# Five Strassen pairs in the longer down part, and an adding DMA for one weight piece of each gate/up chunk

## The chip, the cores and the metric

The kernel runs on one core of a Trainium2 chip, in float32 data. The metric is device time in microseconds (us), lower is better. The kernel before takes 1867.61 us (median of 3 runs, 1867.21 to 1868.33).

## The reference

One transformer layer on 256 tokens of width 2048, all in float32, cut to what matters here:

```python
def swiglu(h, w_gate, w_up, w_down):
    return (jax.nn.silu(h @ w_gate) * (h @ w_up)) @ w_down

def reference(x, positions, ...):
    x = x + 0.5 * swiglu(rmsnorm(x, ffn1_norm), w_gate1, w_up1, w_down1)   # 2048 -> 5632 -> 2048
    h = rmsnorm(x, mix_norm)
    ...   # projections of h, rope, retention, sparse attention -> ro, ao
    x = x + concatenate([ro, ao], axis=-1) @ w_out
    x = x + 0.5 * swiglu(rmsnorm(x, ffn2_norm), w_gate2, w_up2, w_down2)
    return rmsnorm(x, final_norm)
```

## The kernel before, in words

**Precision.** Each weight and each activation is split into a rounded part `hi` and a remainder `lo = raw - hi`. A product of two blocks is three matmuls (hi with hi, hi with lo, lo with hi), each of a 128x128 left block with 512 columns. ScalarE (ACT) writes `hi` (line 287), VectorE (DVE) writes `lo` (line 293).

**Pairs.** The large products go through `wide`. A chunk of 1024 output columns is worked off in pairs of weight rows (2 x 128 rows), one pair a load of 1 MB. A "C" pair makes eight block products, 24 matmuls, in two pieces of 12. An "S" pair makes seven products after Strassen and Winograd, 21 matmuls, in four pieces of 6, 6, 6 and 3; for it DVE forms four differences of weight blocks (`less`, line 279) and later recombines the seven sums. The left blocks of an S pair cost more too: `left_pair` makes four sums by `blocks_of` (lines 320 to 329) where a C pair has one split (lines 341 and 342), and it takes two tiles of the pool `mid` where a C pair takes one.

**A gate/up chunk** covers 512 hidden columns of gate and of up. Chunk 0 of each of the two FFNs has C pairs alone ("plain"); chunks 1 to 10 follow `UP` in the order S C S C S C C C, which is 22 pieces: 0 to 3 are the first S pair, 12 to 15 the third, 16 and 17, 18 and 19, 20 and 21 the three C pairs at the end (pair five, six and seven, counted from 0). The FFN runs in two parts: chunks 0 to 5, then the longer down part (`DOWN[0]`, 12 pairs for each half of the output), then chunks 6 to 10 and the shorter down part.

**Order.** Every engine works off its instructions in the order in which the program issues them, which is written out by hand. For step i the program first runs what is due at i (`run_step`), then issues `split(i + 4)`, the hi and lo of a piece four ahead, then the matmuls of piece i. Raw loads have three buffers and are issued by SyncE (SP) from `split`: on the first piece of load j, load j + 2 is issued, and it waits until the pieces of load j - 1 have been split. hi and lo have five buffers each. Things due: at step 16 of a chunk (`s_end`) `sums_of` begins: ACT copies bank M1 (line 482), DVE adds bank M6 to it (line 477). At step 17 TensorE (PE) turns the hidden values of the chunk before, four 128x128 transposes into M1 and four into M6 (line 567), so these wait for the copy and for the addition. At step 21 and at the next chunk's step 0, `ups` and `hidden` finish the chunk on DVE and ACT.

**Other places that the change touches.** `tables` makes the rope tables in two passes, one after the other, from the start of the first FFN's longer down part; `turn_early` turns x into four banks at the end of the first FFN; `row_of` and `scaled_tables` make a row of reciprocal norms and scale the tables with it; `ret_mix(3)` makes the last retention block for the output product; FIRST is the order of the first chunk's pairs, for each of which x is split, with more work for pairs 1, 3 and 5.

Of the kernel before, what the change touches and what calls it, by code (L numbers as in the profile page):

```python
# [19 lines left out]
P = 128  # L20
# [8 lines left out]
UP = "CSCSCSCC"  # L29
ORDER = (1, 0, 3, 2, 5, 4, 6, 7)  # L30
PLAIN = "CCCCCCCC"
FIRST = (0, 2, 4, 6, 7, 1, 3, 5)
DOWN = ("SCSCSCSCCCCC", "SCSCSCSCCC")
NH = 8
NI = 16
TOPK = 64
# [15 lines left out]
def layer(ctx: ExitStack, tc: tile.TileContext, a: dict, out: bass.AP):  # L52
# [2 lines left out]

    one = ctx.enter_context(tc.tile_pool(name="one", bufs=1))
    wts = ctx.enter_context(tc.tile_pool(name="wts", bufs=4))
    mid = ctx.enter_context(tc.tile_pool(name="mid", bufs=16))
    tmp = ctx.enter_context(tc.tile_pool(name="tmp", bufs=2))
    dram = ctx.enter_context(tc.tile_pool(name="dram", bufs=1, space=bass.MemoryType.DRAM))  # L60
    psum = ctx.enter_context(tc.tile_pool(name="psum", bufs=1, space=PSUM))
# [9 lines left out]
    def half_k(tag, bufs=2):  # L71
        return new(tmp, [P, 2, T], F32, tag, bufs)
# [35 lines left out]
    def after(step, fn):  # L108
        ends.setdefault(step, []).append(fn)
# [68 lines left out]

    def wide(src, plan, left, x0=False, tail=False, order=None, sums=SUM):

        start = len(pieces)
        seen, last = {}, {}
        ending = [[], []]
        s_end = None

        def mm(i, off, a, m, at=None, p=None):

            for n, (u, v) in enumerate(((0, 0), (0, 1), (1, 0))):
                st = m not in seen
                seen[m] = 1  # L190
                e = [i, off, (pieces[i]["pair"], a), m, u, v, st, False]
                last[m] = e
                pieces[i if at is None else at]["mms"].append(e)

        for at, p in enumerate(order or range(len(plan))):
            kind = plan[p]
            loads.append([(0, block(src, 2 * at, 2 * at + 2, 1024))])
            if x0:
                loads[-1] = [lambda p=p: load_xT(p)] + [(o, loads[-1][0][1][:, o:o + n]) for o, n in
                                                        ([(0, 512), (512, 512), (1024, 1024)] if at == 0 else [(0, 2048)])]  # L200
            i = len(pieces)
            if kind == "C":
                tiles = [(0, 1024), (1024, 1024)]
                if x0 and at == 0:
                    tiles = [(0, 512), (512, 512), (1024, 1024)]
            else:
                tiles = [(512, 1024), (1024, 1024), (0, 1024), (1536, 512)]
            for k, (off, n) in enumerate(tiles):
                pieces.append(dict(load=len(loads) - 1, off=off, n=n, mms=[], left=left, pair=p,
                                   sums=k if kind == "S" else None, x=[p] if x0 and k == 0 else []))  # L210
            if kind == "C":
                for c in (1, 0):
                    for k in range(2):
                        off = 1024 * (1 - c) + 512 * k
                        j = max(j for j, (o, n) in enumerate(tiles) if o <= off)
                        for t in range(2):
                            if tail and p >= len(plan) - 2:
                                ending[t].append((i + j, off - tiles[j][0], p, (t, k), sums[f"{t + 1}{c + 1}"]))
                                continue
                            mm(i + j, off - tiles[j][0], (t, k), sums[f"{t + 1}{c + 1}"])  # L220
            else:
                for k, off, a, m in S_BLOCKS:
                    mm(i + k, off, a, m)
                s_end = len(pieces)

        ending[1].sort(key=lambda e: e[4], reverse=True)
        for t in range(2):
            for i, off, p, a, m in ending[t]:
                mm(i, off, a, m, i if t == 0 else len(pieces) - 1)
        for e in last.values():  # L230
            e[7] = True
        return start, s_end, len(pieces) - 1, len(pieces)
# [22 lines left out]
        return len(pieces)  # L255

    n_loaded = [0]

    def load(i):
        raws[i] = new(wts, [P, 2048], F32, "raw", 3)  # L260
# [7 lines left out]
    def split(i):  # L268
        p = pieces[i]
        while n_loaded[0] < min(len(loads), p["load"] + 3):  # L270
            load(n_loaded[0])
            n_loaded[0] += 1
        for c in p.get("x", []):
            first_x(c, xT.pop(c))
        r = raws[p["load"]]
        raw = r[:, p["off"]:p["off"] + p["n"]]

        def less(a, b, o):
            V.tensor_tensor(r[:, o:o + 512], r[:, a:a + 512], r[:, b:b + 512], op=OP.subtract)  # L279


        k = p.get("sums")
        if k == 1:
            less(0, 1024, 1024)
        hi = new(wts, [P, 1024], F32R, "hi", BUFS)
        lo = new(wts, [P, 1024], F32R, "lo", BUFS)
        S.activation(hi[:, :p["n"]], raw, AF.Copy)  # L287
        if k == 1:
            less(0, 512, 0)
            less(512, 1024, 512)  # L290
        elif k == 2:
            less(1536, 512, 1536)
        V.tensor_tensor(lo[:, :p["n"]], raw, hi[:, :p["n"]].bitcast(F32), op=OP.subtract)  # L293
        split_of[i] = (hi, lo)


    def gain(norm, c, j):
# [141 lines left out]
    def row_of(tok):  # L439

        diag = new(tmp, [P, 2, P], F32, "diag", 1)
        for t in range(2):
            V.tensor_scalar(diag[:, t], ident, tok[:, t:t + 1], None, op0=OP.mult)
        ps = small()
        yield 2
        for t in range(2):
            TE.matmul(ps[:, t * P:(t + 1) * P], lhsT=ones, rhs=diag[:, t], start=True, stop=True)
        return ps[:, :T]
# [77 lines left out]
    def ffn(which, norm, next_norm, last):  # L526
        wgu, wd = a[f"wgu{which}"], [a[f"wd{which}{j}"] for j in range(2)]
        c = 0
        for part, n in enumerate(PARTS):
            hs = {}  # L530
            marks[which, part] = len(pieces)
            for cc in range(n):
                plain = c == 0
                start, s_end, half, end = wide(wgu[c], PLAIN if plain else UP, left_of(xg if plain else xs),
                                               plain and which == 1,
                                               order=ORDER if not plain else FIRST if which == 1 else None)
                u = {}

                if not plain:
# [51 lines left out]

    def turn_early(s_end, norm):

        for i, m in enumerate(("M1", "M5", "M6", "M7")):
            after(s_end + 2 + i, lambda i=i, m=m: turn_x(i, norm, m))

    def turn_late(end, norm, banks, later=0):
# [49 lines left out]

    rot_dram = new(dram, [P, 4, T], F32, "rot_dram")

    def tables():  # L650
        for k in range(2):
            ang, n = half_k("b"), half_k("sq")
            pi, pf = n[:, 0].bitcast(I32), n[:, 1]
            G.dma_start(pi, bass.AP(tensor=a["pos"].tensor, offset=a["pos"].offset, ap=[[0, P], [1, T]]))
            yield 4
            V.tensor_copy(pf, pi)
            for j in range(2):
                V.tensor_scalar(ang[:, j], pf, inv[:, k:k + 1], None, op0=OP.mult)
            yield 2
            V.tensor_scalar(n, ang, 1.0 / C_TWO_PI, None, op0=OP.mult)  # L660
            V.tensor_scalar(n[:, 0], n[:, 0], 0.25, None, op0=OP.add)
            yield 2
            V.tensor_scalar(n, n, MAGIC, None, op0=OP.add)
            V.tensor_scalar(n, n, MAGIC, None, op0=OP.subtract)
            for c in (C1, C2, C3):
                yield 2
                V.scalar_tensor_tensor(ang, n, -c, ang, op0=OP.mult, op1=OP.add)
            yield 1
            V.tensor_scalar(ang[:, 0], ang[:, 0], math.pi / 2, None, op0=OP.add)
            yield 1  # L670

            V.tensor_scalar(n, ang, 1.0 / C_TWO_PI, MAGIC, op0=OP.mult, op1=OP.add)
            V.tensor_scalar(n, n, MAGIC, None, op0=OP.subtract)
            for c in (C1, C2, C3):
                yield 2
                V.scalar_tensor_tensor(ang, n, -c, ang, op0=OP.mult, op1=OP.add)
            yield 2
            V.tensor_scalar(ang, ang, PI_DOWN, -PI_DOWN, op0=OP.min, op1=OP.max)
            yield 2
            S.activation(ang, ang, AF.Sin)  # L680
            yield 2
            V.tensor_scalar(ang[:, 1], ang[:, 1], sgn[:, k:k + 1], None, op0=OP.mult)
            G.dma_start(rot_dram[:, 2 * k:2 * k + 2], ang)
        yield 1
        act_table(AF.Silu)

    def load_tables():
        mix_ext()
# [12 lines left out]

    after(FIRST_SQ, first_squares)
    end = ffn(1, 0, 1, False)
    after(marks[1, 0, "down"] + 1, tables)
    after(marks[1, 1, "down"] + 4, load_tables)


# [6 lines left out]
        yield 2  # L714
        V.tensor_tensor(rot[:, :2], rot[:, :2], two(r_of[1]), op=OP.mult)

    after(m0 + 3, scaled_tables)

    heads = {}
    done_at = {}  # L720
# [26 lines left out]
    def cols(name, src, nchunks, idx=False, first=False):  # L747
# [7 lines left out]
        for c in range(nchunks):  # L755
# [3 lines left out]
            def done(chunk=chunk, c=c):  # L759
                if c % 2 == 0:  # L760
                    heads[name].append(big(shape=(P, 4, T)))
                return rope(chunk, 2, heads[name][c // 2][:, 2 * (c % 2):2 * (c % 2) + 2], idx,
                            3 if len(heads) == 1 and c == 0 else 1)

            after(end, done)
        done_at[name] = len(pieces)
# [42 lines left out]
    for c in range(4):  # L809
# [3 lines left out]
        def rg_done(chunk=chunk, c=c):  # L813
# [3 lines left out]
            s = half_k("s")  # L817
            S.activation(s, g, AF.Silu)
            gate[c] = s

        after(end, rg_done)
        rg_end.append(end)
# [213 lines left out]
    after(s + 6, ret_norm)  # L1036
    for n in range(2):
        after(s + 7 + n, lambda n=n: ret_scale(n))
    for c in range(4):
        after(max(rg_end[c] + 2, s + 10 + 2 * c), lambda c=c: ret_mix(c))  # L1040

    class MixIn:
# [129 lines left out]
```

## Time and profile before

| | |
|---|---|
| median of 3 runs | 1867.61 us |
| the profiled execution, its own time | 1868.15 us |
| its span, first to last instruction | 1866.3 us |
| busy: PE, DVE, ACT, POOL | 98%, 88%, 57%, 0% |
| granted TensorE clock | 0.997 of full speed |
| DMA engines busy with the loads of weights | 51.6% |

A busy PE counts pipelined matmuls whose ends are modelled, so the share says that PE hardly ever stops, not that it is at its peak. DVE is the engine with the next highest share. In rows of groups the columns are: line, engine, operation, out<-in, shapes, count, busy us, mean ns of one, and idle time before them with what ended it. In timelines: start, duration, engine, line, operation, and in brackets the idle time before it and its releaser.

### The profile page before, as it was taken

The numbers are of one execution on the slowest core, as the hardware profiler recorded it, in microseconds if no ns is written. First come the engines' busy times: TensorE is split into PE (matmuls) and PEld (weight loads), VectorE is DVE, ScalarE is ACT, GpSimd is POOL, SyncE is SP. The second block draws the span as 40 slices with busy tenths as digits, with TensorE's granted clock in tenths as the row PEclk, the third lists the DMA queues.
The fourth block names the chain that finished last, engine by engine and source line by source line (L and its number), as shares of the span: only waits on it lengthen the run. The fifth ranks groups of instructions, "written<-read, shape, count | busy, mean of one in ns | idle before, by whom it ended". The sixth has DMA issues, their size and how long they took to land.

```text
span 1866.3 us, 22800 instructions
## 1 busy us (share of the span) xinstructions
PE 1836.9 (98%) x8643; PEld 1523.8 (82%) x8643; DVE 1646.2 (88%) x2122; ACT 1072.9 (57%) x1353; POOL 6.9 (0%) x17
## 2 busy tenths in 40 slices
PE   9999999999999999999999999999999999999997
PEld 7788787888888887988888888888888888888886
DVE  6999999999999997689865886799999889999997
ACT  7655655545565555656554566556555455555564
POOL 0000000000000000000000000000000000000000
PEclk9999999999999999999999999999999999999999
DMA  8545555565554544545434464555555555555454
GB/s 316 203 181 183 203 203 191 180 229 198 205 206 183 212 181 173 184 159 210 179 137 172 145 225 150 207 185 191 210 207 183 202 203 198 186 188 212 186 190 170
DMA packets 52237, 360.51 MB, mean 193 GB/s; under 512 B 5984, under 2 KB 5984, under 8 KB 9632
## 3 DMA queue, kind: packets, MB, share of 16 engines
q1 hardware_dynamic: 50976, 355.62, 51.6%
q0 software_dynamic: 576, 1.84, 0.3%
q10 hardware_dynamic: 576, 1.60, 0.3%
q8 instruction: 67, 1.10, 0.2%
q14 instruction: 42, 0.34, 0.1%
HBM read 356.42 MB, written 2.62 MB: 192 GB/s over the span
## 4 chain that ended last, share of the span: by engine, by line
PE 80%; DVE 12%; ACT 4%; issue 2%; DMA 2%; SPq 0%; ACTq 0%; DVEq 0%
PE M L236 63%; PE M L150 8%; DVE lo L293 7%; PE M L152 4%; DVE raw L279 2%; ACT hi L287 2%; PE M L168 1%; PE M L169 1%; PE M L167 1%; PE M L567 1%; DMA raw<-in_wgu 1%; DMA e<-in_xT 1%; DVE x L474 1%; ACT sq L416 0%; DVE e L477 0%
## 5 line engine op out<-in xcount | busy, mean ns | idle before, releaser
L287 ACT ACTIVATE hi<-raw 128x1024 fp32r<-128x1024 f32 (+2 forms) x859 | 844.6, 1006 | 561.5 <-DVE raw L279 359.5
L293 DVE TENSOR_TENSOR lo<-raw,hi 128x1024 fp32r<-128x1024 f32 (+2 forms) x859 | 976.4, 1159 | 122.1 <-ACT hi L287 108.7
L236 PE MATMUL M<-hi,xg 128*128 128x512 f32 x2240 | 725.5, 390 | 1.7 <-ACT e L546 1.5
L236 PE MATMUL M<-hi,mid 128*128 128x512 f32 x1690 | 527.4, 391 | 1.9 <-DVE e L1001 1.6
L236 PEld LDWEIGHTS M<-hi,xg 128*128 128x128 f32 x2240 | 420.5, 188 | 89.2 <-ACT e L546 1.9
L236 PE MATMUL M<-lo,xg 128*128 128x512 f32 x1120 | 437.9, 391 | 5.7 <-DVE lo L293 5.6
L236 PEld LDWEIGHTS M<-hi,mid 128*128 128x128 f32 x1690 | 317.2, 188 | 70.2 <-DVE e L1001 2.0
L236 PE MATMUL M<-lo,mid 128*128 128x512 f32 x845 | 329.8, 390 | 1.0 <-DVE lo L293 0.8
L279 DVE TENSOR_TENSOR raw<-raw 128x512 f32<-128x512 f32 x380 | 262.9, 692 | 12.7
L236 PEld LDWEIGHTS M<-lo,xg 128*128 128x128 f32 x1120 | 210.3, 188 | 55.5 <-DVE lo L293 12.7
L150 PE MATMUL M<-xg,hi 128*128 128x512 f32 x688 | 245.6, 401 | 0.4 <-DVE xg L307 0.3
L236 PEld LDWEIGHTS M<-lo,mid 128*128 128x128 f32 x845 | 158.6, 188 | 36.5 <-DVE lo L293 4.3
L152 PE MATMUL M<-xg,lo 128*128 128x256 f32 x645 | 180.9, 280 | 0.0
L150 PEld LDWEIGHTS M<-xg,hi 128*128 128x128 f32 x688 | 128.7, 189 | 30.3 <-issue 1.3
L236 PE MATMUL M<-hi,ext 128*128 128x512 f32 x360 | 141.2, 392 | 1.5 <-ACT s L557 1.4
L152 PEld LDWEIGHTS M<-xg,lo 128*128 128x128 f32 x645 | 122.3, 190 | 0.8
L236 PEld LDWEIGHTS M<-hi,ext 128*128 128x128 f32 x360 | 67.5, 188 | 18.9 <-DVE s L477 3.6
L236 PE MATMUL M<-lo,ext 128*128 128x512 f32 x180 | 70.1, 389 | 0.0
L477 DVE TENSOR_TENSOR s<-s,M 128x512 f32<-128x512 f32 x98 | 65.6, 683 | 1.9 <-PE M L236 0.9
L557 ACT ACTIVATE s<-s,r_tok 128x512 f32<-128x512 f32 x40 | 27.0, 718 | 53.5 <-DVE s L477 53.5
L477 DVE TENSOR_TENSOR e<-s,M 128x512 f32<-128x512 f32 x58 | 39.7, 684 | 1.0
L742 ACT ACTIVATE b<-e 64x512 f32<-64x512 f32 (+2 forms) x46 | 28.1, 612 | 19.8 <-DVE e L728 19.3
(176 smaller groups left out, 933.2 us busy)
## 6 DMA issues: line engine op xcount, KB each, us to landing
raw<-in_wgu SPq DMA_DIRECT2D x175, 1024.0 KB, 4.8
raw<-in_wd SPq DMA_DIRECT2D x88, 1024.0 KB, 4.8
raw<-in_w_out SPq DMA_DIRECT2D x16, 1024.0 KB, 4.9
raw<-in_w_iq SPq DMA_DIRECT2D x8, 1024.0 KB, 4.8
raw<-in_w_aq SPq DMA_DIRECT2D x8, 1024.0 KB, 4.7
raw<-in_w_rk SPq DMA_DIRECT2D x8, 1024.0 KB, 4.8
raw<-in_w_rq SPq DMA_DIRECT2D x8, 1024.0 KB, 4.7
raw<-in_w_rv SPq DMA_DIRECT2D x8, 1024.0 KB, 4.9
```

The lines of the kernel that those rows point to most:

```text
L150: TE.matmul(acc, lhsT=hi[:, c:c + P], rhs=r, start=st, stop=sp)
L152: TE.matmul(acc[:, T:], lhsT=lo[:, c:c + P], rhs=r[:, :T], start=False, stop=False)
L167: TE.matmul(o, lhsT=h, rhs=hi[:, i * n:(i + 1) * n], start=st, stop=False)
L168: TE.matmul(o, lhsT=h, rhs=lo[:, i * n:(i + 1) * n], start=False, stop=False)
L169: TE.matmul(o, lhsT=l, rhs=hi[:, i * n:(i + 1) * n], start=False, stop=sp)
L236: TE.matmul(bank[m], lhsT=p["left"](pair, a)[u], rhs=split_of[i][v][:, off:off + 512], start=st, stop=sp)
L279: V.tensor_tensor(r[:, o:o + 512], r[:, a:a + 512], r[:, b:b + 512], op=OP.subtract)
L287: S.activation(hi[:, :p["n"]], raw, AF.Copy)
L293: V.tensor_tensor(lo[:, :p["n"]], raw, hi[:, :p["n"]].bitcast(F32), op=OP.subtract)
L477: V.tensor_tensor(o, a, b, op=OP.add)
L557: S.activation(u[b], bank[SUM[b]] if plain else u[b], AF.Silu, scale=r_tok[norm][:, t:t + 1])
L742: S.activation(b[p0:p0 + w], q[p1:p1 + w], AF.Copy)
```

## The change

- `DOWN[0]` has a fifth S pair (pair 8) in place of a C pair. It holds for both halves of the output in both FFNs. The pool `mid` gets a 17th tile, and the scratch of POOL's DMAs is set to 4096 bytes.
- In the twenty gate/up chunks that are not plain, the lo of the last piece (21) is no longer made by DVE. At `split(18)` ACT writes `-hi` of piece 21 into a new tile `lower`, and POOL issues a DMA that adds the raw piece to it.
- Orders and delays: FIRST; the banks of `turn_early`; `row_of` waits 3 steps in place of 2 and `scaled_tables` begins one step later, the first two ropes wait longer; `tables` runs as two chains, 28 and 57 steps after the start of the longer down part, each in fewer and fuller steps and with its own load of the Silu table; `ret_mix(3)` follows its gate directly.

```diff
-FIRST = (0, 2, 4, 6, 7, 1, 3, 5)
-DOWN = ("SCSCSCSCCCCC", "SCSCSCSCCC")
+FIRST = (0, 2, 1, 4, 3, 6, 5, 7)
+DOWN = ("SCSCSCSCSCCC", "SCSCSCSCCC")
...
-    mid = ctx.enter_context(tc.tile_pool(name="mid", bufs=16))
+    mid = ctx.enter_context(tc.tile_pool(name="mid", bufs=17))
...
+        if added:
+            pieces[-4]["lower"] = len(pieces) - 1
+            pieces[-1]["adds"] = True
...
         hi = new(wts, [P, 1024], F32R, "hi", BUFS)
-        lo = new(wts, [P, 1024], F32R, "lo", BUFS)
+        lo = lowers.pop(i) if p.get("adds") else new(wts, [P, 1024], F32R, "lo", BUFS)
         S.activation(hi[:, :p["n"]], raw, AF.Copy)
...
-        V.tensor_tensor(lo[:, :p["n"]], raw, hi[:, :p["n"]].bitcast(F32), op=OP.subtract)
+        if not p.get("adds"):
+            V.tensor_tensor(lo[:, :p["n"]], raw, hi[:, :p["n"]].bitcast(F32), op=OP.subtract)
         split_of[i] = (hi, lo)
+        if p.get("lower"):
+            q = pieces[p["lower"]]
+            src = raws[q["load"]][:, q["off"]:q["off"] + q["n"]]
+            lowers[p["lower"]] = t = new(wts, [P, 1024], F32R, "lower", 1)
+            S.activation(t, src, AF.Copy, scale=-1.0)
+            G.dma_start(t, src, accum_op=OP.add)
...
         ps = small()
-        yield 2
+        yield 3
...
-                                               order=ORDER if not plain else FIRST if which == 1 else None)
+                                               order=ORDER if not plain else FIRST if which == 1 else None,
+                                               added=not plain)
...
-        for i, m in enumerate(("M1", "M5", "M6", "M7")):
+        for i, m in enumerate(("M1", "M6", "M7", "M5")):
             after(s_end + 2 + i, lambda i=i, m=m: turn_x(i, norm, m))
...
-    def tables():
-        for k in range(2):
...
+    def tables(k):
+        ang, n = half_k("b"), half_k("sq")
...
+        S.activation(ang, ang, AF.Sin)
         yield 1
         act_table(AF.Silu)
+        yield 1
+        V.tensor_scalar(ang[:, 1], ang[:, 1], sgn[:, k:k + 1], None, op0=OP.mult)
+        G.dma_start(rot_dram[:, 2 * k:2 * k + 2], ang)
...
-    after(marks[1, 0, "down"] + 1, tables)
+    for k in range(2):
+        after(marks[1, 0, "down"] + (28, 57)[k], lambda k=k: tables(k))
...
-    after(m0 + 3, scaled_tables)
+    after(m0 + 4, scaled_tables)
...
-                            3 if len(heads) == 1 and c == 0 else 1)
+                            (5, 4)[c] if len(heads) == 1 and c < 2 else 1)
...
             gate[c] = s
+            if c == 3:
+                ret_mix(c)
...
-    for c in range(4):
+    assert rg_end[3] + 1 >= s + 16
+    for c in range(3):
         after(max(rg_end[c] + 2, s + 10 + 2 * c), lambda c=c: ret_mix(c))
...
-    nc = bacc.Bacc("TRN2", target_bir_lowering=False, num_devices=1)
+    nc = bacc.Bacc("TRN2", target_bir_lowering=False, num_devices=1, dynamic_dma_scratch_size=4096)
```

## Rows read from the trace of the kernel before

**Rows 1.** The page: busy time of each engine; the chain that ended last.

```profile
PE 1836.9 (98%) x8643; PEld 1523.8 (82%) x8643; DVE 1646.2 (88%) x2122; ACT 1072.9 (57%) x1353; POOL 6.9 (0%) x17
...
PE 80%; DVE 12%; ACT 4%; issue 2%; DMA 2%; SPq 0%; ACTq 0%; DVEq 0%
```

**Rows 2.** Waits of PE: who waited for whom, total us, times, longest us.

```profile
PE M L236 <- DVE lo L293: 6.4, 19, 0.7
PE M L447 <- DVE diag L443: 2.4, 1, 2.4
...
PE M L236 <- DVE e L1001: 1.6, 1, 1.6
PE M L236 <- ACT e L546: 1.5, 1, 1.5
PE M L405 <- DVE e L477: 1.4, 1, 1.4
PE M L236 <- ACT s L557: 1.4, 1, 1.4
```

**Rows 3.** Busy time by window: chunk 3, then the longer down part of FFN 1, FFN 2.

```profile
143.90:187.00 43.10, 42.76 (x193) 34.95 (x192) 41.46 (x51) 25.10 (x31) 0.54 (x1) 1.00 0.53 197
...
273.30:397.00 123.70, 121.46 (x536) 99.06 (x535) 118.17 (x153) 63.46 (x69) 1.63 (x3) 1.00 0.56 205
1413.00:1536.70 123.70, 123.70 (x552) 102.50 (x551) 109.06 (x122) 64.90 (x68) 0.00 (x0) 1.00 0.55 200
```

**Rows 4.** Timeline of PE around the start of chunk 3.

```profile
146.05 0.39 PE L236 MATMUL M<-hi,xg 128*128 128x512 f32 x1
146.78 0.50 PE L236 MATMUL M<-lo,xg 128*128 128x512 f32 x1 [0.34 <-DVE lo L293]
```

**Rows 5.** Groups by line and shape, DVE and ACT.

```profile
L293 DVE TENSOR_TENSOR lo<-raw,hi 128x1024 fp32r<-128x1024 f32 x756 | 910.4, 1221 | 117.7 <-ACT hi L287 104.3
L287 ACT ACTIVATE hi<-raw 128x1024 fp32r<-128x1024 f32 x756 | 783.0, 1056 | 477.6 <-DVE raw L279 293.1 <-PE M L236 112.6 <-PE M L169 21.2
...
L279 DVE TENSOR_TENSOR raw<-raw 128x512 f32<-128x512 f32 x380 | 262.9, 692 | 12.7
...
L293 DVE TENSOR_TENSOR lo<-raw,hi 128x512 fp32r<-128x512 f32 x97 | 66.4, 685 | 2.8 <-ACT hi L287 2.8
```

**Rows 6.** Chain that ended last: a long stretch of matmuls without a wait.

```profile
1449.56 156.43 PE M L236 x690
```

**Rows 7.** Timeline of ACT in chunk 3: hi of piece 18, copy of M1, hi of piece 20.

```profile
165.29 1.06 ACT L287 ACTIVATE hi<-raw 128x1024 fp32r<-128x1024 f32 x1 [0.29 <-PE M L236]
...
167.57 0.58 ACT L482 ACTIVATE s<-M 128x512 f32<-128x512 f32 x1
168.95 1.06 ACT L287 ACTIVATE hi<-raw 128x1024 fp32r<-128x1024 f32 x1 [0.80 <-DVE lo L293]
```

**Rows 8.** Timeline of SP in chunk 3: issue of the load of pieces 20 and 21.

```profile
164.07 0.33 SPq L266 DMA_DIRECT2D raw<-in_wgu  x1
```

**Rows 9.** DMA issues: engine, count, size, median us to landing.

```profile
raw<-in_wgu SPq DMA_DIRECT2D x175, 1024.0 KB, 4.8
...
mid<-in_qdec POOLq DMA_DIRECT2D x1, 512.0 KB, 6.8
```

**Rows 10.** Chain that ended last, chunk 3 of FFN 2: that load, then hi of piece 20.

```profile
1303.56 5.12 DMA raw<-in_wgu
...
1308.79 1.07 ACT hi L287
```

**Rows 11.** Timeline of DVE in chunk 3: the addition of M6.

```profile
168.84 0.68 DVE L477 TENSOR_TENSOR s<-s,M 128x512 f32<-128x512 f32 x1
```

**Rows 12.** Timeline of PE in chunk 3: the eight transposes and the matmul behind them.

```profile
169.81 1.03 PE L567 MATMUL M<-ident,e 128*128 128x128 f32 x8
170.60 0.48 PE L236 MATMUL M<-hi,xg 128*128 128x512 f32 x1
```

**Rows 13.** Chunk 7, where DVE ran early: hi of piece 20; PE's transposes and next matmul.

```profile
467.96 1.05 ACT L287 ACTIVATE hi<-raw 128x1024 fp32r<-128x1024 f32 x1
...
469.72 1.03 PE L567 MATMUL M<-ident,e 128*128 128x128 f32 x8
470.51 0.48 PE L236 MATMUL M<-hi,xg 128*128 128x512 f32 x1
```

More of the change, by code (lines that the diff above doesn't have):

```diff
@@ L177, in layer, with wide @@
         (3, 0, "A22", "M4"))
-    def wide(src, plan, left, x0=False, tail=False, order=None, sums=SUM):
+    def wide(src, plan, left, x0=False, tail=False, order=None, sums=SUM, added=False):
         start = len(pieces)
@@ L208, in wide @@
             for k, (off, n) in enumerate(tiles):
-                pieces.append(dict(load=len(loads) - 1, off=off, n=n, mms=[], left=left, pair=p,
+                pieces.append(dict(load=len(loads) - 1, off=off, n=n, mms=[], left=left, pair=p, lower=None, adds=False,
                                    sums=k if kind == "S" else None, x=[p] if x0 and k == 0 else []))
@@ L257, in layer @@
     n_loaded = [0]
+    lowers = {}
     def load(i):
@@ L648, in layer @@
     rot_dram = new(dram, [P, 4, T], F32, "rot_dram")
-    def tables():
-        for k in range(2):
[L652 to L683, printed above, removed]
@@ new lines, in tables, with less_turns @@
+    def tables(k):
+        ang, n = half_k("b"), half_k("sq")
+        pi, pf = n[:, 0].bitcast(I32), n[:, 1]
+        G.dma_start(pi, bass.AP(tensor=a["pos"].tensor, offset=a["pos"].offset, ap=[[0, P], [1, T]]))
+        yield 2
+        def less_turns(c):
+            V.scalar_tensor_tensor(ang, n, -c, ang, op0=OP.mult, op1=OP.add)
+        V.tensor_copy(pf, pi)
+        for j in range(2):
+            V.tensor_scalar(ang[:, j], pf, inv[:, k:k + 1], None, op0=OP.mult)
+        yield 1
+        V.tensor_scalar(n, ang, 1.0 / C_TWO_PI, None, op0=OP.mult)
+        V.tensor_scalar(n[:, 0], n[:, 0], 0.25, None, op0=OP.add)
+        yield 1
+        V.tensor_scalar(n, n, MAGIC, None, op0=OP.add)
+        V.tensor_scalar(n, n, MAGIC, None, op0=OP.subtract)
+        yield 1
+        less_turns(C1)
+        less_turns(C2)
+        yield 1
+        less_turns(C3)
+        V.tensor_scalar(ang[:, 0], ang[:, 0], math.pi / 2, None, op0=OP.add)
+        yield 1
+        V.tensor_scalar(n, ang, 1.0 / C_TWO_PI, MAGIC, op0=OP.mult, op1=OP.add)
+        V.tensor_scalar(n, n, MAGIC, None, op0=OP.subtract)
+        yield 1
+        less_turns(C1)
+        less_turns(C2)
+        yield 1
+        less_turns(C3)
+        V.tensor_scalar(ang, ang, PI_DOWN, -PI_DOWN, op0=OP.min, op1=OP.max)
+        yield 2
+        S.activation(ang, ang, AF.Sin)
@@ L684, in tables @@
         yield 1
         act_table(AF.Silu)
+        yield 1
+        V.tensor_scalar(ang[:, 1], ang[:, 1], sgn[:, k:k + 1], None, op0=OP.mult)
+        G.dma_start(rot_dram[:, 2 * k:2 * k + 2], ang)
     def load_tables():
```

## The prediction

> **What bounds the kernel now.** I read the busy shares and the chain first. PE is busy 98% of the span and holds 80% of the chain; DVE is busy 88% and holds 12% [rows 1]. So the time is PE's work plus the few places where PE stops, and almost all of these stops end on DVE. Second, the list of PE's waits: one small wait that recurs, DVE's lo, 19 times with 0.7 us at most, and single waits of 1.4 to 2.4 us at lines 447, 1001, 546, 405 and 557 [rows 2]. Third, the windows: in a gate/up chunk PE has 42.76 us of 43.1 and DVE 41.46, so DVE is all but full there; in the longer down part DVE has 118.17 us of 123.7 in the first FFN, where the rope tables are made, and 109.06 in the second, where they are not [rows 3]. Last, the timeline at the start of a chunk: the matmul with the lo of piece 4 starts 0.73 us after the one before it, where 0.23 is usual, a stop of 0.5 us [rows 4]. In the timeline this stop follows sixteen of the twenty chunks (1 to 4 and 7 to 10 of both FFNs): DVE leaves the end of a chunk, with the sums and the hidden values in it, about that late. It is what the adding DMA is aimed at.
>
> **The fifth S pair.** It removes 3 matmuls for each of two halves in two FFNs, 12 in all. A long stretch ran 690 matmuls in 156.43 us, 0.227 us each [rows 6], so PE is given back **2.7 us**. DVE gets four differences of 0.692 us and 1.5 more lo pieces (1.22 and 0.685): 4.7 us a pair, 9.4 us for each FFN's down part [rows 5]; ACT gets 1.5 hi pieces and has room (57%) [rows 1]. In the second FFN 109.06 + 9.4 = 118.5 us fits into 123.7 - 1.4 = 122.3 [rows 3]: no cost; the cover there is DVE's idle time. The pair's left blocks add sums and splits of some 2 us to DVE in one chunk of each FFN, in the place where DVE loses a lo of 1.22 us; I put that at nothing and let the bounds hold it.
>
> **The tables.** In the first FFN 118.17 + 9.4 = 127.6 us of DVE stands against 122.3 of PE. DVE is short by 5.3 us, and the two chains are put into the tails behind the last S pair of each half, where the recombining and the additions to x already stand, in some thirteen steps each where there were over twenty. I take **+6 us**, near the shortfall, because DVE won't work without any pause; the ends are 0, if the lead with which DVE leaves the part pays for all of it, and 11, if DVE keeps the 5.5 us of idle time that it has now [rows 3].
>
> **The adding DMA: what it gives.** DVE loses one lo of 1.22 us in each of twenty chunks, ACT gains one copy of 1.06 [rows 5]. The 0.5 us stops go, since DVE comes 1.2 us earlier to a place where it is 0.5 late: 16 x 0.5 = **-8 us**.
>
> **The adding DMA: what it costs.** The copy of -hi for piece 21 is issued by split(18), so it stands on ACT behind hi of piece 18 and ahead of hi of piece 19 and the copy of bank M1. It reads the load of pieces 20 and 21. In chunk 3 that load is issued at 164.07 [rows 8] and takes 4.8 us [rows 9]: it lands at 168.9. The chain shows the same in the second FFN: the load, 5.12 us, then hi of piece 20 0.1 us behind [rows 10]. Yet hi of piece 18 ends at 166.35, and the copy of M1 runs at 167.57, before the load has landed; hi of piece 20 starts at 168.95 [rows 7], as soon as it has (the view names DVE's lo there, but the landing is the later). So the new copy can't start before 168.95, and all behind it on ACT waits: 168.95 + 1.06 for it, 1.06 for hi of piece 19, then on DVE, which works in order too, 1.22 for lo of piece 19 and 0.68 for the addition of M6 [rows 5, 11]: 172.97. Today that addition ends at 169.52, just ahead of the eight transposes, whose second half needs it. The transposes take 0.79 us [rows 12]; half of them after 172.97 let the next product start at 173.4 in place of 170.60: PE stops for 2.8 us. In chunk 7, where DVE ran early, the same sum is 467.96 + 1.06 + 1.06 + 1.22 + 0.68 + 0.4 = 472.4 against 470.51 [rows 13]: 1.9 us. The ends are 1.9 and 2.8; with a lo less DVE will run like the early case, so I take 2.0. The load can't come much sooner: its buffer comes free with lo of piece 15, and from the chunk's start to there DVE is full with work that the change leaves alone. Transposes stand at that step in chunks 1 to 5 and 7 to 10 (chunk 6 follows the down part and has none), 18 in all: 18 x 2.0 = **+36 us**.
>
> The Trainium skill, in "PSUM — Partial Sum Buffer", section "Engine vs sequencer instructions", says that the queues of ScalarE and VectorE are strictly first in, first out. By that rule the 36 us stand; were it otherwise they would be nought. No row here shows an instruction overtaking another, and none shows one that could have.
>
> **The DMA itself.** No row shows an adding DMA. POOL's load of 512 KB took 6.8 us [rows 9]; an add reads two sides, so between 6.8 and twice that, 13.6. The copy ends at 170.0; PE wants piece 21's lower part after four more pieces of 12 matmuls, at 173.4 + 4 x 2.72 + 0.2 = 184.5: 14.5 us of cover, so nothing at either end, and I take 6.8. Behind it on SP stands the load that reuses that buffer, for pieces 6 to 9 of the next chunk; it would be issued at 177 to 184 and land 4.8 us later, and it is first read at about 189. POOL itself has 17 busy instructions in the whole span [rows 1], and no one waits behind it.
>
> The Trainium skill prices such a DMA lower ("DMA: Bandwidth & Descriptors", section "Anatomy of one DMA — SWDGE (gpsimd) path"): about 2 us and the bytes at 436 GB/s, an estimate of 3.2 us for 512 KB. The row is twice that; by the page the sum would be the same, with more cover.
>
> **The orders.** Each is priced by the wait that it can remove [rows 2]. turn_early: M5 is freed last and is now used last, -1.4 (line 405). The norm row: its matmul comes two steps, some 5 us, later, -2.4 (line 447); the ropes that follow have their own waits lengthened. ret_mix(3) stands ahead of a split on DVE, -1.6 (line 1001). FIRST: the work on x for pairs 1, 3 and 5 is spread, so the two waits of 1.5 and 1.4 at the end of chunk 0 (lines 546, 557) shrink; the Silu table load that sits between them stays, so I take half, -1.5. Together **-6.9 us**, with 0 as the other end, since a wait that goes may come back at the next instruction.
>
> **Sum.** 1868.15 (the profiled execution's own time) + 36 - 8 - 2.7 + 6 - 6.9 = 1892.6. The median of the runs is 0.5 us lower, so **1892 us**, 1.3% slower.
>
> **The rivals.**
> (a) The copy doesn't hold PE up: the load lands earlier than I think relative to ACT, or the transposes have other slack. Then the 36 us fall away: 1867.6 - 8 - 2.7 + 6 - 6.9 = 1856. For it: DVE, which frees the load's buffer, is relieved. Against it: hi of piece 20, which reads the same load, starts on the landing in chunk 3 of both FFNs, in the first 2.6 us after hi of piece 18 ended [rows 7, 8, 10]. It decides once the landing comes before the end of hi of piece 18. Chance 0.13.
> (b) The DMA is late: three passes instead of two make 20.4 us, 5.9 more than the cover, in each of twenty chunks: +118, about 2010. For it: nothing shows its speed, and it shares the engines with loads. Against it: 52% of the engines' time is used. Chance 0.06.
> (c) The wait is at its lower end, the tables fit, and the small ones give all they can, with further waits that I can't see shrinking: 1867.6 + 18 x 1.9 - 8 - 2.7 - 6.9 = 1884, and it takes 0.7 us less per chunk still to come within 0.2% of no change. That margin of 0.2%, 3.7 us, is about what a measurement of this kernel can tell. Chance of "same" 0.06.
>
> **How the numbers follow.** The forecast has 0.75, and with (b) slower has 0.81; faster 0.13; same 0.06. The forecast's own range is 1884 to 1867.6 + 18 x 2.8 - 8 - 2.7 + 11 = 1918. To hold the time 8 times in 10 it is taken down to 1867, through (c) and the same case; (a) and (b) are left out.
>
> **What would show it.** In the changed kernel PE should wait for DVE at line 477 some 18 times for about 2 us, and the recurring wait for lo of piece 4 should be gone; ACT's new copy should start on the landing of the load, 2 us after hi of piece 18. The down part of the first FFN should hold new waits for DVE in its two tails; the waits at lines 447, 405 and 1001 should be gone. I am wrong if the transposes of a chunk start as soon as the matmuls ahead of them end, or if the adding DMA lands after piece 20.

## The result and the profile after

The changed kernel takes **1898.12 us** (median of 4 runs, 1897.58 to 1899.25) against 1867.58 before (4 runs): ratio 1.0162, 95% interval 1.0149 to 1.0174, 30.5 us slower. Its profiled execution spans 1896.4 us, at a granted clock of 0.994 (0.997 before).

Lines of the code have moved: the split is now L291 (hi) and L298 (lo), the copy of -hi L304 and its DMA L305, the copy of bank M1 L493, the additions of sums L488, the additions to x L485, the transposes of a chunk L579, the matmuls of `wide` L239, those of a projection L150 and L152.

The page of after, busy time and the chain that ended last (before: [rows 1]):

```profile
PE 1840.0 (97%) x8631; PEld 1526.0 (80%) x8631; DVE 1642.0 (87%) x2136; ACT 1102.5 (58%) x1386; POOL 24.5 (1%) x37
...
PE 61%; DVE 26%; DMA 5%; issue 5%; ACT 3%; SPq 0%; ACTq 0%; DVEq 0%
```

PE's share of the chain fell from 80% to 61% and DVE's rose from 12% to 26%, though DVE has 4 us less to do. So it is not work that was added; somebody waits. The waits of PE say for whom (before: [rows 2]; who waited for whom, total us, times, longest us):

```profile
PE M L579 <- ACT s L493: 16.5, 18, 1.3
PE M L579 <- DVE s L488: 12.9, 18, 0.7
PE M L239 <- DVE x L485: 8.1, 3, 5.9
PE M L150 <- DVE xg L318: 4.2, 1, 4.2
PE M L239 <- DVE lo L298: 2.4, 5, 0.9
...
```

The waits for lo went from 19 to 5. In their place the transposes wait 18 times for the copy of M1 and 18 times for the addition of M6, 29.4 us in all. (The list counts idle time after a matmul's modelled end, so it holds somewhat less than PE loses.) Two more are new: 5.9 us for an addition to x, and 4.2 us for a turned tile of x at the projections. The first two are seen on ACT in chunk 3 (timeline; before: [rows 7]; in square brackets the idle time ahead of the instruction, and who ended it):

```profile
165.79 1.06 ACT L291 ACTIVATE hi<-raw 128x1024 fp32r<-128x1024 f32 x1 [0.29 <-PE M L239]
168.83 1.06 ACT L304 ACTIVATE lower<-raw 128x1024 fp32r<-128x1024 f32 x1 [1.97 <-DMA raw<-in_wgu]
169.80 1.04 ACT L291 ACTIVATE hi<-raw 128x1024 fp32r<-128x1024 f32 x1
170.74 0.58 ACT L493 ACTIVATE s<-M 128x512 f32<-128x512 f32 x1
```

and on PE (timeline; before: [rows 12]):

```profile
170.08 0.39 PE L239 MATMUL M<-hi,xg 128*128 128x512 f32 x1
171.37 0.66 PE L579 MATMUL M<-ident,e 128*128 128x128 f32 x4 [0.91 <-ACT s L493]
172.75 0.66 PE L579 MATMUL M<-ident,e 128*128 128x128 f32 x4 [0.72 <-DVE s L488]
173.16 0.47 PE L239 MATMUL M<-hi,xg 128*128 128x512 f32 x1
```

The copy starts on the landing, 1.97 us after ACT had nothing else ahead of it. hi of piece 19 and the copy of M1 need nothing from that load, yet they stand behind it. The Trainium skill ("PSUM — Partial Sum Buffer", section "Engine vs sequencer instructions") calls these queues strictly first in, first out; this trace agrees, with hi of piece 19 at 169.80 right behind the copy. On PE the eight transposes, one run before, are split into two fours with a stop ahead of each.

The period of a chunk is read from the copy of M1: its first and last start over chunks 1 to 5 (one line of code on ACT; copies, durations in ns, first and last start), before:

```profile
L482 ACT ACTIVATE s<-M x5: 576/578/580, 81.3 to 253.9; 128x512 f32<-128x512 f32 x5
```

and after:

```profile
L493 ACT ACTIVATE s<-M x5: 576/577/577, 81.9 to 259.7; 128x512 f32<-128x512 f32 x5
```

(253.9 - 81.3) / 4 = 43.15 us became (259.7 - 81.9) / 4 = 44.45, 1.3 more a chunk: the wait's cost less what the DMA gives. The same reading from chunk 5 to chunk 6 holds the longer down part of the first FFN: 253.9 to 426.0 before, 172.1 us; 259.7 to 442.3 after, 182.6.

### The profile page after: what moved, and what is told of

Its sections match the earlier page's. It is cut to its first block, busy times and chain, and to the rows that moved or that the text cites. A ratio compares the mean times of both kernels' runs of the same rounds, so it can differ in the third digit from the quotient of the medians.

```text
span 1896.4 us, 22945 instructions
## 1 busy us (share of the span) xinstructions
PE 1840.0 (97%) x8631; PEld 1526.0 (80%) x8631; DVE 1642.0 (87%) x2136; ACT 1102.5 (58%) x1386; POOL 24.5 (1%) x37
## 4 chain that ended last, share of the span: by engine, by line
PE 61%; DVE 26%; DMA 5%; issue 5%; ACT 3%; SPq 0%; ACTq 0%; DVEq 0%
PE M L239 42%; DVE lo L298 15%; PE M L150 9%; DVE raw L283 7%; DMA raw<-in_wgu 5%; PE M L152 4%; ACT hi L291 2%; DVE x L485 1%; DVE s L488 1%; PE M L168 1%; PE M L169 1%; PE M L167 1%; PE M L579 1%; DVE e L488 1%; ACT sq L427 0%
## 5 line engine op out<-in xcount | busy, mean ns | idle before, releaser
L291 ACT ACTIVATE hi<-raw 128x1024 fp32r<-128x1024 f32 (+1 forms) x867 | 856.2, 1006 | 518.3 <-DVE raw L283 362.0
L298 DVE TENSOR_TENSOR lo<-raw,hi 128x1024 fp32r<-128x1024 f32 (+1 forms) x847 | 960.8, 1155 | 157.0 <-ACT hi L291 142.3
L239 PE MATMUL M<-hi,xg 128*128 128x512 f32 x2240 | 726.5, 390 | 5.9 <-DVE x L485 5.9
L239 PE MATMUL M<-hi,mid 128*128 128x512 f32 x1682 | 527.1, 391 | 2.7 <-DVE x L485 2.3
L239 PEld LDWEIGHTS M<-hi,xg 128*128 128x128 f32 x2240 | 421.0, 188 | 93.2 <-DVE x L485 6.3
L239 PE MATMUL M<-lo,xg 128*128 128x512 f32 x1040 | 405.4, 390 | 0.8 <-DVE lo L298 0.7
L239 PEld LDWEIGHTS M<-hi,mid 128*128 128x128 f32 x1682 | 316.3, 188 | 72.2 <-DVE x L485 6.4
L239 PE MATMUL M<-lo,mid 128*128 128x512 f32 x841 | 328.5, 391 | 1.7 <-DVE lo L298 1.7
L283 DVE TENSOR_TENSOR raw<-raw 128x512 f32<-128x512 f32 x396 | 274.1, 692 | 13.3
L150 PE MATMUL M<-xg,hi 128*128 128x512 f32 x688 | 246.5, 402 | 4.2 <-DVE xg L318 4.2
L239 PEld LDWEIGHTS M<-lo,xg 128*128 128x128 f32 x1040 | 195.6, 188 | 41.6 <-DVE lo L298 1.6
L239 PEld LDWEIGHTS M<-lo,mid 128*128 128x128 f32 x841 | 158.2, 188 | 36.3 <-DVE lo L298 4.2
L152 PE MATMUL M<-xg,lo 128*128 128x256 f32 x645 | 181.5, 281 | 0.0
L150 PEld LDWEIGHTS M<-xg,hi 128*128 128x128 f32 x688 | 129.3, 189 | 34.1 <-DVE xg L318 4.6
L239 PE MATMUL M<-hi,ext 128*128 128x512 f32 x360 | 140.5, 390 | 0.7 <-ACT s L569 0.7
L152 PEld LDWEIGHTS M<-xg,lo 128*128 128x128 f32 x645 | 122.9, 190 | 0.7
L239 PEld LDWEIGHTS M<-hi,ext 128*128 128x128 f32 x360 | 67.7, 188 | 15.5 <-ACT s L569 1.1
L239 PE MATMUL M<-lo,ext 128*128 128x512 f32 x180 | 70.0, 389 | 0.0
L488 DVE TENSOR_TENSOR s<-s,M 128x512 f32<-128x512 f32 x98 | 65.2, 683 | 1.0
L579 PE MATMUL M<-ident,e 128*128 128x128 f32 x176 | 27.7, 284 | 29.4 <-ACT s L493 16.5
L579 PEld LDWEIGHTS M<-ident,e 128*128 128x128 f32 x176 | 18.8, 140 | 41.7 <-ACT s L493 22.4
```

The lines of the kernel that those rows point to most:

```text
L150: TE.matmul(acc, lhsT=hi[:, c:c + P], rhs=r, start=st, stop=sp)
L152: TE.matmul(acc[:, T:], lhsT=lo[:, c:c + P], rhs=r[:, :T], start=False, stop=False)
L239: TE.matmul(bank[m], lhsT=p["left"](pair, a)[u], rhs=split_of[i][v][:, off:off + 512], start=st, stop=sp)
L488: V.tensor_tensor(o, a, b, op=OP.add)
L579: TE.transpose(v[:, j, t * P:(t + 1) * P], ht[t][:, halves(2 * q + j, P)], ident)
```

## The experiments

Each time below stands against the runs of the kernel before on the same chip (1867.1, 1866.8 and 1867.75 us in the three sets). In the expectations W is the theory that ACT, waiting for the landing, holds up what is queued behind it; its rivals, B and D, put the cost on the new work itself, ACT's copy and the DMA's traffic. All edits are to the changed kernel where nothing else is said.

**The copy two pieces later**

```diff
-            pieces[-4]["lower"] = len(pieces) - 1
+            pieces[-2]["lower"] = len(pieces) - 1
```

> The changed kernel with one edit: the copy of -hi and the adding DMA for piece 21 are issued by the split of piece 20, behind its hi, in place of piece 18. Theory W (the copy holds ACT until its load has landed, and the transposes wait behind it): the copy now stands behind an instruction that waits for the same load anyway; the 18 waits of 1.07 + 0.86 us go, and 1898 falls by 34.7 to 1863 us (1860 to 1867). Theory B (what costs is ACT's extra 1.06 us and the added instructions, wherever they stand): 1898 within 3. Theory D (the adding DMA costs, by its traffic or by coming late): 1898 or more, since it now ends later and nearer to its use.

Measured 1861.70 us, ratio 0.9970 (0.9958 to 0.9982), inside W's range and 36.4 us less than after. The same copies and the same DMAs, issued at split(20), where hi of piece 20 has had to wait for that load anyway. ACT's timeline in chunk 3:

```profile
162.85 1.06 ACT L291 ACTIVATE hi<-raw 128x1024 fp32r<-128x1024 f32 x1 [0.25 <-PE M L239]
163.82 0.57 ACT L493 ACTIVATE s<-M 128x512 f32<-128x512 f32 x1
164.55 1.06 ACT L291 ACTIVATE hi<-raw 128x1024 fp32r<-128x1024 f32 x1 [0.16 <-DMA raw<-in_wgu]
165.52 1.04 ACT L304 ACTIVATE lower<-raw 128x1024 fp32r<-128x1024 f32 x1
```

The copy of M1 now comes ahead of the landing, and no wait of PE at L579 is left. W holds, and B and D, which leave the time at 1898, fall.

**The copy where it was, from a load that has landed** (it reads the load of its own piece 18; so one product of piece 21 takes another remainder)

```diff
-            src = raws[q["load"]][:, q["off"]:q["off"] + q["n"]]
+            src = raws[p["load"]][:, q["off"]:q["off"] + q["n"]]
```

> The changed kernel, with the copy and the adding DMA at the split of piece 18 as they are, but both read piece 19's half of the load that is already there in place of piece 21's; so one of the three products of the last piece of twenty chunks takes a wrong remainder. Same instructions, same places, same sizes, only no wait for a landing. Theory W: 1863 us (1860 to 1867). Theories B and D: 1898 within 3, since ACT's work and the DMA's traffic are all there.

Measured 1861.42 us, 0.9968 (0.9955 to 0.9981). The copy stands at split(18), ahead of hi of piece 19 as in the change, and costs nothing there once its data is in. So the cost is the wait for the landing alone, and not the copy, its place or the DMA.

**The copy with its wait, no DMA**

```diff
-        lo = lowers.pop(i) if p.get("adds") else new(wts, [P, 1024], F32R, "lo", BUFS)
+        lo = new(wts, [P, 1024], F32R, "lo", BUFS)
...
-        if not p.get("adds"):
+        if True:
...
-            G.dma_start(t, src, accum_op=OP.add)
```

> The changed kernel without the adding DMA: ACT's copy stays at the split of piece 18 and waits for the load of pieces 20 and 21, nobody reads it, and DVE makes the lo of piece 21 again. Theory W: the waits stay, and since DVE is as late as in the kernel before, each may grow from 1.9 to 2.8 us: 1898 to 1914. Theory D: the time falls to 1863 to 1875. Theory B: 1898 plus up to 10 for the stops on DVE that come back.

Measured 1922.39 us, 1.0295 (1.0280 to 1.0310), 24.3 us over after. Without the DMA's relief the small waits for lo come back, and the wait for the copy grows. PE's waits (the lines behind the DMA's stand one higher here):

```profile
PE M L578 <- ACT s L492: 21.0, 18, 1.5
PE M L578 <- DVE s L487: 12.9, 18, 0.7
...
PE M L239 <- DVE lo L298: 5.7, 17, 0.8
```

These are 4.5 + 3.3 = 7.8 us more than after, and the time 24.3. The granted clock of this run is 0.987, yet a slower clock is not what lengthens the chunks. Chunk 3 shows it, where the clock fell behind the stops of 1.36 and 0.72 us. Two windows, from one copy of M1 to the next (length, busy time of PE, PEld, DVE, ACT and POOL, then granted clock, DMA share, GB/s), and the three copies of M1:

```profile
127.80:173.50 45.70, 43.30 (x191) 34.93 (x191) 41.37 (x51) 25.93 (x31) 0.00 (x0) 1.00 0.49 185
173.50:219.20 45.70, 44.35 (x191) 36.32 (x191) 41.46 (x51) 26.31 (x32) 0.00 (x0) 0.96 0.49 181
```

```profile
127.79 0.58 ACT L492 ACTIVATE s<-M 128x512 f32<-128x512 f32 x1
173.50 0.58 ACT L492 ACTIVATE s<-M 128x512 f32<-128x512 f32 x1
219.17 0.58 ACT L492 ACTIVATE s<-M 128x512 f32<-128x512 f32 x1
```

45.71 us with the clock at 1.00 and 45.67 with 0.96: the fall made the chunk no longer. What each chunk has more than in after is 45.70 - 44.45 = 1.25 us. That is about the one lo of 1.22 us [rows 5] which DVE makes again in each of the twenty, 24.4 in all; the match is one of numbers, no run shows it by itself. The run was over every theory's range. W's, 1898 to 1914, let the waits grow and forgot that the DMA's relief goes with the DMA: 14.4 us by the next run, and with it the range would have been 1912 to 1928. Against that next run, which has neither copy nor DMA, the copy's wait costs 1922.4 - 1876.1 = 46.3 us, 2.6 a place, within the prediction's 1.9 to 2.8.

**No adding DMA, the rest of the change**

```diff
-                                               added=not plain)
+                                               added=False)
```

> The changed kernel without copy and adding DMA in all chunks; the fifth S pair, the tables and the orders stay. It prices the rest of the change. If the adding DMA costs 18 x 1.93 and gives 16 x 0.5 (theory W): 1898 - 34.7 + 8 = 1871, 3.7 us above the kernel before, most of it in the longer down part of the first FFN. If the rest gave what the prediction took for it (+6 - 2.7 - 6.9), 1864.

Measured 1876.08 us, 1.0047 (1.0031 to 1.0064): a rest that was thought to cost little costs 9.0 us by itself. It is 5 us over the 1871 that were expected, which took the DMA's relief at 8 us: against the late copy, the adding DMA in a good place is worth 1876.1 - 1861.7 = 14.4 us.

**The order of the turned x.** Late copy, and the bank M5 third instead of last:

```diff
-        for i, m in enumerate(("M1", "M6", "M7", "M5")):
+        for i, m in enumerate(("M1", "M6", "M5", "M7")):
```

> The kernel with the late copy (1861.7 us), and one more edit: the early turns of x go to the banks M1, M6, M5, M7 in place of M1, M6, M7, M5. Theory T: the wait of 4.3 us at the start of the projections is for bank M5, which the last of the four turns holds and the first projection chunk writes; with M5 one turn earlier and M7 last (its next writer comes two pieces, some 5 us, later) it goes: 1857 to 1859 us. Rival: that wait is for DVE's late split of x itself, whatever bank it sits in: no change, 1862.

Measured 1857.92 us, 0.9949 (0.9934 to 0.9964): 3.5 us better than the late copy, both against their own chip. The first chunk of the projections takes the pair M5 and M6. With M5 turned last, it waited 4.2 us for the evacuation of that tile; 1.1 is left. The change had moved the wait of [rows 2] at line 405 to where it was three times as long.

**The tables, and the fifth pair.** On top of the last kernel: the tables as they were before; four S pairs with the new tables; four S pairs with the old tables.

```diff
-    for k in range(2):
-        after(marks[1, 0, "down"] + (28, 57)[k], lambda k=k: tables(k))
+    after(marks[1, 0, "down"] + 1, tables)
...
```

```diff
-DOWN = ("SCSCSCSCSCCC", "SCSCSCSCCC")
+DOWN = ("SCSCSCSCCCCC", "SCSCSCSCCC")
```

> The kernel with the late copy and the turn order M1, M6, M5, M7, and the rope tables made as in the kernel before: one chain from the start of the longer down part. Theory S (the place of the tables in the tails costs): the waits of 2.2, 1.3 and 6.0 us of the first FFN's down part go, 10 us with what stands around them, and 3 to 6 us come back in the first half's S region, where the kernel before lost 2.9: 4 to 7 us less than the same kernel with the new tables. Theory F (DVE has too much work there with five S pairs, wherever it stands): within 2 us of it.

> The kernel with the late copy, the turn order M1, M6, M5, M7 and the new tables, but with the fourth S pair as the last in the longer down part, as in the kernel before. Theory S: the tails stay overfull only in part, since they are now ten steps long; the waits of 10 us shrink to 3 or less, 2.7 us of matmuls come back: 4 to 8 us less than with five. Theory F: the same sign. If the fifth pair pays for itself even so, 2.7 us more.

> The kernel with the late copy and the turn order M1, M6, M5, M7, four S pairs and the old tables: the kernel before with a well placed adding DMA and the small orders. Sum: 1867.1 - 16 x 0.6 for the stops, - 2.4 for the norm row, - 1.5 for the start, - 1.4 for the turn: 1852 us. If this is the fastest of the four, the fifth S pair and the new tables cost more than they give.

Measured 1852.88 (0.9922, 0.9907 to 0.9936), **1849.04** (0.9902, 0.9885 to 0.9918) and 1849.56 us (0.9906, 0.9891 to 0.9921). With five pairs the old tables take 5.0 us less than the new: theory S, which had 4 to 7, holds, and F, which had at most 2, falls. The fifth pair costs 8.9 us with the new tables, 0.9 over the range of S, and still 3.3 with the old ones, so the place of the tables is not all of it: the pair takes matmuls out and loses time. The third kernel came out 2.4 us under its sum of 1852. Chunk 5 to chunk 6 of the first FFN, read from the copy of M1, first with five pairs and the new tables, then with four:

```profile
L493 ACT ACTIVATE s<-M x4: 576/576/579, 249.6 to 431.3; 128x512 f32<-128x512 f32 x4
```

```profile
L493 ACT ACTIVATE s<-M x4: 572/576/577, 249.2 to 421.6; 128x512 f32<-128x512 f32 x4
```

181.7 us against 172.4, the whole difference; with the old tables the same reading gives 176.3 and 172.0. The new tables by themselves are no gain with four pairs (1849.0 and 1849.6 can't be told apart). In the second FFN, which makes no tables, five pairs against four give 168.0 and 168.4 us.

**The adding DMA alone, in the kernel before**, at split(20) and at split(18). The edit is that of the change, with the scratch of 4096 bytes, and nothing else of it.

> The kernel before with the adding DMA alone, its copy at the split of piece 20 as in the late copy; none of the fifth pair, the tables or the orders. If the adding DMA is worth what the two kernels with and without it differ by in the changed kernel (1876.1 - 1861.7 = 14.4 us), this one takes 1867 - 14 = 1853 us, range 1851 to 1855. The run with four S pairs and old tables (1849.6) has this edit and the orders, so the difference to it is the orders by themselves: -6.9 us by the prediction, so that this one would take 1856; -3 us or so if the orders give less, and the two agree within 1 us if they give nothing.

> The kernel before with the adding DMA alone, but at the split of piece 18 as in the change. The prediction's own terms say +36 - 8, so 1867 + 28 = 1895 us. The measured wait alone (after less late copy, 1898.1 - 1861.7 = 36.4 us over 20 chunks) above the kernel of this job with the late copy gives 1853 + 36 = 1889 us. If the wait needs the busier down part or the orders of the change to show, this one stays within 10 us of the late one.

Measured 1855.70 us late, 0.9936 (0.9919 to 0.9953), 12.0 us faster; and 1894.42 us early, 1.0141 (1.0126 to 1.0156), 26.7 us slower. The early one came out at the 1895 of the prediction's own terms. The late one missed its range by 0.7: in a kernel without the rest of the change the relief is worth 12, not 14. The copy of M1 in chunks 1 to 5, late and then early:

```profile
L493 ACT ACTIVATE s<-M x5: 575/577/577, 82.4 to 251.9; 128x512 f32<-128x512 f32 x5
```

```profile
L493 ACT ACTIVATE s<-M x5: 575/577/578, 84.6 to 262.2; 128x512 f32<-128x512 f32 x5
```

Periods of 42.38 and 44.40 us, against 43.15 before and 44.45 after: the early copy alone makes the period of the changed kernel, 2.0 us a chunk above the late one. PE's waits in the early one show the pair of after (the nineteenth of the second line, 2.0 us, is one that the kernel before has too):

```profile
PE M L579 <- ACT s L493: 15.6, 18, 1.4
PE M L579 <- DVE s L488: 14.9, 19, 2.0
```

**The orders alone, in the kernel before** (four S pairs, old tables, no adding DMA; the bank order of the change; the 17th tile of `mid` and the scratch of 4096 bytes stay)

> The kernel before with the orders of the change alone (first chunk's pairs, norm row, first rope, gate mix, turned x with the bank order of the change): no adding DMA, four S pairs, the old tables. By the prediction -6.9 us: 1860. By the trace of after: norm row, gate mix and first chunk give about -4 to -5, the turned x takes away 1.5 and puts 4.3 to 4.7 in its place, so 1865 to 1866, within 0.2% of before.

Measured 1864.39 us, 0.9986 (0.9977 to 0.9996), 3.4 us faster, a little more than expected: the 2.4 us at the norm row and the 1.6 at the gate mix are gone, the two waits at chunk 0 (1.5 and 1.4 [rows 2]) are down to one of 0.6, and 4.2 at the projections have come. With the bank order mended and the late copy, the orders give 17.2 - 12.0 = 5.2 us (four S pairs with old tables against the late DMA alone).

**All that paid, together.** Late copy, mended bank order, four S pairs in the first FFN and five in the second, tables from pieces 20 and 50 on:

```diff
-DOWN = ("SCSCSCSCSCCC", "SCSCSCSCCC")
+DOWN = {1: ("SCSCSCSCCCCC", "SCSCSCSCCC"), 2: ("SCSCSCSCSCCC", "SCSCSCSCCC")}
...
-        after(marks[1, 0, "down"] + (28, 57)[k], lambda k=k: tables(k))
+        after(marks[1, 0, "down"] + (20, 50)[k], lambda k=k: tables(k))
```

> The late copy and the mended bank order, four S pairs in the first FFN's longer down part and five in the second's, the tables begun at pieces 20 and 50 of the down part, not 28 and 57. Against the run with four S pairs in both (1849.0): the second FFN gives 0.4 us by the run with five; the stops of 1.57 and 0.34 us at the second half and of 0.59 and 0.37 at the next chunk go if the vector engine's work for the tables no longer falls on the additions there. So 1846 to 1849; over 1850 if the moved tables only collide elsewhere.

Measured **1846.65 us**, 0.9885 (0.9870 to 0.9900), 21.1 us faster than before, as expected and faster than both kernels. What PE still waits for:

```profile
PE M L239 <- DVE lo L298: 2.2, 5, 0.8
PE M L150 <- DVE xg L318: 1.1, 1, 1.1
PE M L652 <- DVE ones L650: 1.1, 1, 1.1
PE M L239 <- DVE x L485: 0.7, 2, 0.4
...
```

Not tried: the 17th tile of `mid` and the smaller scratch each by itself, and the new start of the tables without the second FFN's fifth pair.

## Why the prediction was right, point by point

The sign, the size and the mechanism came true: 1892 forecast, 1898 measured, inside the forecast's own range of 1884 to 1918. Summed from the runs, the early DMA alone is +26.7 and the orders alone -3.4; what is left of 30.5 for the fifth pair and the tables is +7.2. That the sum came within 6 us is in part luck: the DMA gave 4.0 more than forecast and the orders 3.5 less, and the two cancel.

| term | forecast, us | measured, us | by |
|---|---|---|---|
| the adding DMA gives | -8 | -12.0 | late DMA alone against before |
| its copy's wait costs | +36 | +38.7; 36.4 | early against late alone; after against the late copy |
| orders | -6.9 | -3.4 | orders alone |
| fifth pair and tables | +3.3 | +7.2 | the rest; 8.4 with the late copy (1857.9 - 1849.6); 12.4 without copy and DMA (9.0 + 3.4) |
| all | +24.4 | +30.5 | after against before |

- **The copy waits for the landing, and the copy of M1, lo and the addition of M6 behind it.** Right in each step. The sum of the prediction for chunk 3 put the copy at 168.95 and the next product at 173.4; they came at 168.83 and 173.16. That both fit so well is in part luck. PE is half a us later there than in before: the last product ahead of the transposes starts at 170.08, where the transposes themselves started at 169.81 [rows 12]. Without a stop the next product would have come at 170.08 + 0.23 + 0.79 = 171.1, so the stop is 2.1 us and not the 2.8 of that sum. The 18 places are there, and the step is by far the largest term. With 2.0 us a place (the distance of the two periods, 44.40 - 42.38) the lower part of its range was the right one, as the prediction chose from chunk 7. Rival (a) needed the landing ahead of the end of hi of piece 18, at 166.85 in after: it is 2 us behind it. The second run shows what (a) would have been, 1861.4 for the forecast's 1856.
- **What the DMA gives** was mis-sized: 16 stops x 0.5 = 8, measured 12.0. The period falls by 43.15 - 42.38 = 0.77 a chunk and not by 0.5. The stop for the lo of piece 4 [rows 4] was the largest of the small losses at a chunk's start, and I had counted that one alone. In before the product behind it is late too, and so is one shortly before it in the next chunk (timeline of PE in before):

```profile
147.11 0.63 PE L236 MATMUL M<-hi,xg 128*128 128x512 f32 x2
...
186.37 0.50 PE L236 MATMUL M<-hi,ext 128*128 128x512 f32 x1
186.70 0.39 PE L236 MATMUL M<-lo,ext 128*128 128x512 f32 x1
```

  From 146.78 to 147.11 and from 186.37 to 186.70 are 0.33 us each, 0.1 more than the usual 0.23; with the late DMA alone neither is late.
- **The DMA is hidden:** right. It was guessed from POOL's plain load at 6.8 us; the row of after:

```profile
lower<-raw POOLq DMA_DIRECT2D x20, 512.0 KB, 4.8
```

  In chunk 3 it was issued at 170.19 and landed at 175.4, some 9 us before piece 21 was due; rival (b) falls. The estimate worked out from the Trainium skill ("DMA: Bandwidth & Descriptors", section "Anatomy of one DMA — SWDGE (gpsimd) path") was 3.2 us; the row is 1.6 over it. It took 6.3 and 6.5 us in the first two experiments, where it was as well hidden.
- **The fifth pair in the second FFN:** the cover held, but 0.4 us came of the 1.4 that PE saves.
- **The tables in the first FFN:** the step that failed most. I took the shortfall of DVE, 5.3 us, and +6. The upper end, 11, was for a DVE that keeps the 5.5 us of idle time it had, and that is nearly what it did. Two kernels with the late copy show it free of the early one's wait. From the copy of M1 of chunk 5 to that of chunk 6, which holds the whole longer down part, with four pairs and the old tables, then with five and the new:

```profile
249.00:421.00 172.00, 169.75 (x752) 139.13 (x751) 161.19 (x204) 90.96 (x100) 3.09 (x5) 1.00 0.56 203
249.60:431.30 181.70, 171.10 (x747) 139.82 (x746) 172.66 (x221) 96.25 (x107) 3.08 (x5) 0.98 0.52 193
```

  DVE has 11.5 us more to do, 2.1 over the 9.4 that I took (I had put the left blocks' sums, some 2 us, at nothing), and the stretch is 9.7 us longer: of 10.8 us of idle time 9.0 stay. In after the same stretch is 182.6, against 172.1 before and 175.4 with the early DMA alone (262.2 to 437.6), so that 7.2 of its 10.5 us are the fifth pair and the tables. The new waits are in the two tails, as forecast (2.1 us at 341.5 and 5.9 at 413.4 in after). At the end of the part the additions to x stand on DVE behind the tables' work (L669, L695) and the split, and chunk 6 can't begin (timeline of DVE in after):

```profile
409.85 0.69 DVE L669 SCALAR_TENSOR_TENSOR b<-sq,b 128x512 f32<-128x512 f32 x1
410.56 0.43 DVE L695 TENSOR_SCALAR b<-b 128x512 f32<-128x512 f32 x1
...
412.64 1.28 DVE L485 SCALAR_TENSOR_TENSOR x<-M,x 128x512 f32<-128x512 f32 x2
```

  Windows of after: chunk 3, the start of chunk 6, and the start of the projections:

```profile
143.90:188.30 44.40, 42.77 (x193) 35.01 (x192) 40.20 (x51) 26.16 (x31) 0.86 (x1) 1.00 0.58 200
...
407.00:420.00 13.00, 7.15 (x26) 5.46 (x25) 12.79 (x18) 6.43 (x8) 0.55 (x1) 0.74 0.29 93
...
745.00:750.00 5.00, 5.00 (x16) 4.23 (x17) 3.56 (x4) 1.20 (x2) 0.00 (x0) 0.50 0.47 175
```

  At the start of chunk 6 DVE is busy 12.79 of 13 us and PE 7.15. With the four pairs this stop is gone.
- **turn_early, -1.4:** wrong in sign. I asked which bank is freed last, and not who takes the banks next: that cost 3.5 us by the run that puts it right. It is the step of the orders that failed. The norm row and the gate mix came out as priced, so the orders together gave half.
- **The wait at line 477** stands in the list as two, for ACT's copy of M1 and DVE's addition; I had named the second alone.

## What to carry to other kernels

An instruction that waits for a transfer belongs behind everything in its queue that doesn't: two steps later the same copy turned 1.4% slower into 0.6% faster. Before a product is traded for vector work, look at the end of that stage and not at its mean: a vector engine with 5 us of idle time in 124 hardly gave it up, and the trade cost 3 to 9 us where it was full, by where the other work stood, and paid 0.4 where it was not. When a bank is handed on, look up who asks for it next.

## What the runs showed that I had not expected

PE's clock falls after a long stop. The timeline of PE in after, around the stop at the start of chunk 6, and two windows behind it:

```profile
407.14 0.39 PE L239 MATMUL M<-hi,ext 128*128 128x512 f32 x1
413.38 0.79 PE L239 MATMUL M<-hi,xg 128*128 128x512 f32 x1 [5.85 <-DVE x L485]
...
415.26 0.63 PE L239 MATMUL M<-lo,xg 128*128 128x512 f32 x1
415.68 0.63 PE L239 MATMUL M<-hi,xg 128*128 128x512 f32 x1
...
416.99 0.39 PE L239 MATMUL M<-hi,xg 128*128 128x512 f32 x1
417.21 0.39 PE L239 MATMUL M<-lo,xg 128*128 128x512 f32 x1
```

```profile
413.40:416.40 3.00, 3.00 (x7) 2.42 (x8) 3.00 (x5) 1.56 (x3) 0.00 (x0) 0.50 0.21 44
416.90:420.00 3.10, 3.10 (x16) 2.56 (x15) 2.99 (x4) 1.06 (x1) 0.55 (x1) 1.00 0.86 285
```

After 5.85 us without a matmul they start 0.42 us apart (415.26, 415.68), at a granted clock of 0.50, and 0.22 apart again from 416.99 on, at 1.00: 1.2 GHz first, then 2.4. At the projections, after the 4.2 us stop, the window from 745 to 750 has a granted clock of 0.50, 1.2 GHz throughout, with PE busy all of it. Stops of 0.91 and 0.72 us cost no clock in chunk 3 of after (1.00), while ones of 1.36 and 0.72 were followed by a fall in chunk 3 of the run without the DMA.

A fall need not cost time. In that chunk it cost none (45.71 and 45.67 us). At the projections it seems to: from the last copy of M1 in the first FFN to the next one are 384.3 us with the late copy (704.5 to 1088.8) and 380.1 with the bank order mended too (705.9 to 1086.0), 4.2 less, and PE's listed waits went from 4.2 to 1.1 and 0.3, which is 2.8 less. The other 1.4 us are about what the slow clock took; this is worked out, not measured by a run of its own. The prediction priced no stop this way, and how large a share of the tables' cost lies here stays open.
